# Feed-forward half of one trunk layer: output projection by chunks of 512 tokens, and three groups of the up projection begun with one chunk's products

## The chip, the cores and the metric

The kernel runs on one core of a Trainium2 chip. The metric is the device time of one execution in microseconds: 2342.04 us, the median of 3 runs (2341.98 to 2343.08). The engines are named as the profile names them: PE multiplies matrices into PSUM (8 banks of 128 x 512 float32), DVE and ACT work element by element, SP issues the DMAs, POOL does almost nothing here.

## The reference, cut to what is computed

One layer (`DEPTH = 1`) over 2048 latent tokens of width 1024: a bidirectional RG-LRU mixer of width 1280, then a SwiGLU feed-forward network of width 2816. Everything is float32. What matters here is the end of the mixer and the network behind it:

```
y = (rec * gelu(h @ w_gate)) @ w_out                    # 1280 -> 1024, the output projection
x = x + mx[2] * y
h = rms_norm(x, norm_ffn_g) * (1 + mx[4]) + mx[3]
a, b = split(h @ ffn_w_gu)                              # 1024 -> 2 x 2816, the up projection
x = x + mx[5] * ((silu(a) * b) @ ffn_w_down)            # 2816 -> 1024, the down projection
```

## The kernel before, in words

Tensors are kept transposed: features on the 128 partitions, tokens along the free dimension. The 2048 tokens are four chunks of C = 512, numbered 0 to 3. A float32 product is made of three matmuls on split operands (`mm3`, lines 103 to 109): each operand is a high part, rounded by ACT (line 83), and a low part, the rest, subtracted by DVE (line 84). A pair of weight or data tiles of 128 x 1024 that is loaded and split this way is called a **unit** (`unit`, line 96): one load of 512 KB on SP's queue, one cast, one subtraction.

`sweep1` computes the mixer. `sweep2` (line 1003), to which the change is confined, handles the chunks in two **supers**, (3, 2) and then (1, 0). For the first super:

- `w_out` (line 831) is the output projection of both chunks together. For each half `dg` of the 8 feature tiles it takes 8 banks, 4 per chunk, and runs over 5 steps `j`; a step loads one unit of weights and one unit of input per chunk (`rows`, line 816), 30 units for the super. Each bank is then scaled and added to x on DVE (line 843), stored to `d_x1` and squared and summed for the norm (lines 847 to 851).
- `norm2_bc` (line 854) turns the sums of squares of one chunk into a broadcast row: four small matmuls, 15 tiny DVE operations, one diagonal, one matmul, one copy.
- `combos` (line 865), called for k = 0 to 3, reloads tiles k and k + 4 of both chunks from `d_x1`, scales them (line 881), and makes the seven operands T0 to T6 of a scheme that gets the two chunks' products with both halves of the features in seven products instead of eight. T0 and T1 depend on the first chunk alone, T2 on the second alone, T3 to T6 on both. Each has a high part (ACT, lines 890 and 893) and a low part (DVE, lines 891 and 894). Four differences are formed on DVE (lines 904 to 908).
- `up` (line 935) runs over 22 groups `f`. `up_weights` (line 914) loads two weight tiles, forms four sums of them and splits the results into four operand tiles. Each group has seven products of 12 matmuls, numbered as T, into three banks: `be` collects products 0, 5, 6 and 3, and is copied out by ACT after 0, 5 and 6 (s1, s2, s3); `ep` collects 4 and 2; `al` has product 1. The order in the code is 0, 4, 5, 1, 6, then product 0 of the next group, 3, 2. SiLU and two multiplications give the two chunks' activations, which go to `d_act`.
- Beside `up` of the first super, `back_units` finishes the mixer for chunks 1 and 0 after every second group (a hook), with activations that need other function tables. Beside `down` of the first super the combinations of the second super are made.

Then follow `down` for chunks 3 and 2, `up` of the second super without a hook, and `down` for chunks 1 and 0.

The order of the instructions of each engine is not written out by hand in `sweep2`: a list scheduler at compile time orders them by readiness and priority, and assigns buffers as they come free. Loads and splits of units and weights are given a priority 200 places ahead of their place in the code (`w_off`, line 1059). The buffers that matter: 4 raw tiles (`RAWS`, loads and weight sums), 6 operand tiles (`OPS`, split results), 10 `ld` tiles and 6 `e` tiles of 128 x 512, 28 T tiles, 8 PSUM banks.

Of the kernel before, what the change touches and what calls it, by code (L numbers as in the profile page):

```python
# [12 lines left out]
P = 128  # L13
# [6 lines left out]
T = 2048  # L20
# [11 lines left out]
WS = 9  # L32

# [11 lines left out]
class Trunk:  # L45
# [770 lines left out]
    def rows(self, ps, w_src, x_srcs, name, after=None):  # L816

        m = len(w_src)
        for j in range(m):
            w = self.unit(w_src[j], f"w{name}_{j}")  # L820
            for q, x_src in enumerate(x_srcs):
                x = self.unit(x_src[j].rearrange("p a t -> p (a t)"), f"x{name}_{j}_{q}")
                for i in range(4):
                    for a in range(2):
                        ws, xs = slice(a * C + i * P, a * C + (i + 1) * P), slice(a * C, (a + 1) * C)
                        self.mm3(ps[q][i], (w[0][:, ws], w[1][:, ws]), (x[0][:, xs], x[1][:, xs]),
                                 j == a == 0, j == m - 1 and a == 1)
            if after:
                after(j)

    def w_out(self, s):

        nc = self.nc
        acc = [self.tile2("acc", f"acc{c}") for c in s]
        for dg in range(2):
            ps = [[self.bank(f"ps_wo{c}_{dg}{i}") for i in range(4)] for c in s]
            self.rows(ps, [self.io["w_out"][dg, j] for j in range(NB // 2)], [self.d_rg[c] for c in s], f"o{s[0]}_{dg}")
            for q, c in enumerate(s):
                for i in range(4):
# [3 lines left out]
                    nc.vector.scalar_tensor_tensor(out=x1, in0=ps[q][i], scalar=self.modv[:, d : d + 1], in1=x1,  # L843
                                                   op0=ALU.mult, op1=ALU.add)
                    nc.sync.dma_start(self.d_x1[c][:, d, :], x1)
                    if d == 0:
                        nc.scalar.activation(acc[q], x1, AF.Square)
                    else:
                        sq = self.tile2("e", f"sq{c}_{d}")
                        nc.scalar.activation(sq, x1, AF.Square)  # L850
                        nc.vector.tensor_tensor(out=acc[q], in0=acc[q], in1=sq, op=ALU.add)
# [13 lines left out]
    def combos(self, s, k, bc):  # L865
# [3 lines left out]
        nc = self.nc  # L869
        v = nc.vector  # L870
        sh = lambda j: self.modv[:, 8 + j : 9 + j]
# [3 lines left out]
        x = {}  # L875
        for r in range(2):
            for q in range(2):
                j = k + 4 * r
                t = self.tile2("ld", f"x1n_{s[q]}_{j}")
                nc.sync.dma_start(t, self.d_x1[s[q]][:, j, :])  # L880
                v.scalar_tensor_tensor(out=t, in0=t, scalar=self.A2[:, j : j + 1], in1=bc[q],
                                       op0=ALU.mult, op1=ALU.mult)
                x[r, q] = t
        T = []

        def part(i, src, bias=None):
            t = self.hp.tile([P, 2, C], F32R, tag="T", name=f"T{s[0]}_{k}_{i}", bufs=28)
            h, l = t[:, 0, :], t[:, 1, :]
            if bias is None:
                nc.scalar.copy(h, src)  # L890
                v.tensor_tensor(out=l, in0=src, in1=h.bitcast(F32), op=ALU.subtract)
            else:
                nc.scalar.activation(h, src, AF.Identity, bias=bias, scale=1.0)
                v.scalar_tensor_tensor(out=l, in0=src, scalar=bias, in1=h.bitcast(F32),
                                       op0=ALU.add, op1=ALU.subtract)
            T.append(t)

        b1, b2 = sh(k), sh(k + 4)
        part(0, x[0, 0], b1)
        part(1, x[1, 0], b2)  # L900
        part(2, x[1, 1], b2)
        e = lambda n: self.tile2("e", f"{n}_{s[0]}_{k}")
        t1, t2, t4 = e("t1"), e("t2"), e("t4")
        v.tensor_tensor(out=t1, in0=x[0, 1], in1=x[0, 0], op=ALU.subtract)
        v.scalar_tensor_tensor(out=t2, in0=x[1, 1], scalar=b2, in1=t1, op0=ALU.add, op1=ALU.subtract)
        v.scalar_tensor_tensor(out=t4, in0=x[1, 0], scalar=b2, in1=t2, op0=ALU.add, op1=ALU.subtract)
        t3 = x[0, 1]
        v.scalar_tensor_tensor(out=t3, in0=x[1, 1], scalar=self.shd[:, k : k + 1], in1=t3,
                               op0=ALU.add, op1=ALU.subtract)
        for i, t in ((3, t4), (4, t1), (5, t2), (6, t3)):  # L910
            part(i, t)
        return T

    def up_weights(self, s, f):
# [4 lines left out]
        with self.tc.high_priority(offset=self.w_off):  # L919
# [4 lines left out]
            lo, hi = slice(0, C), slice(C, 2 * C)  # L924
            tt = v.tensor_tensor
            tt(out=sums[:, lo], in0=b[:, lo], in1=b[:, hi], op=ALU.add)
# [3 lines left out]
            pa, ps, pb = (self.parts(t, f"{n}{tag}") for n, t in (("a", a), ("s", sums), ("b", b)))  # L930
            p4 = self.parts(s4, f"s4{tag}", C)
        part = lambda t, o: (t[:, 0, o], t[:, 1, o])
        return [part(pa, lo), part(pa, hi), part(p4, lo), part(pb, hi), part(ps, lo), part(ps, hi), part(pb, lo)]

    def up(self, s, T, hook):
# [4 lines left out]
        v = nc.vector  # L940

        def product(ps, A, i, first):
            for k in range(4):
                ks = slice(k * P, (k + 1) * P)
                x = T[k][i]
# [3 lines left out]
        def add(t, ps):  # L949
            v.tensor_tensor(out=t, in0=ps, in1=t, op=ALU.add)  # L950
# [166 lines left out]
```

## Time and profile before

| | us |
|---|---|
| median of 3 runs | 2342.04 |
| the profiled execution | 2343.92 |
| its span, first to last instruction | 2342.2 |
| PE busy | 2253.5 |
| DVE busy | 1489.7 |
| ACT busy | 1156.4 |
| mean granted clock of PE (1 is full) | 0.975 |

The profiled execution is 1.88 us above the median, and its span 1.7 us shorter than its time. The first super's output projection runs from 721.6 to 836 us, its up projection to 1331, the second super's output projection to 1430, the two down projections to 1680, the second up projection to 2110, the last two down projections to the end. Busy time of PE is modelled from pipelined matmuls; how many were issued in a stretch, and the granted clock, say more than its share.

### The profile page before, as it was taken

To read this page: it belongs to the slowest core of one execution; us is meant where nothing else is said; L and a number is where in the kernel's file an instruction comes from. 1 tells how busy PE (TensorE), PEld (TensorE's weight loads), DVE (VectorE), ACT (ScalarE), POOL (GpSimd) and SP (SyncE) were. 2 spreads that over 40 slices of the span, in tenths; PEclk is the share of its full clock that TensorE was granted. 3 is DMA by queue.
4 is the path that set the end of the run, shared out by engine and by line. 5 is a ranking of instruction groups with operands and counts; after the bars stand their busy time and mean duration, and the time that the engine had idled before them with its cause. 6 is when DMAs were issued, how large, how long until landed. Compare 5 with 4: busy or idle time off the path is not lost.

```text
span 2342.2 us, 25844 instructions
## 1 busy us (share of the span) xinstructions
PE 2253.5 (96%) x9852; PEld 1852.4 (79%) x9852; DVE 1489.7 (64%) x1912; ACT 1156.4 (49%) x1399; POOL 0.7 (0%) x6
## 2 busy tenths in 40 slices
PE   8899999899999958999999999999999999999999
PEld 8578887688887846878787888778888888888887
DVE  4567888678887577676666546864555555545443
ACT  2357775687776335565646334443333333333332
POOL 0000000000000000000000000000000000000000
PEclk9799999999999978999999999999999999999999
DMA  7135555221114733434343666776422222236664
GB/s 280 41 140 207 204 178 207 85 73 63 63 63 154 250 127 112 150 127 164 126 163 121 204 227 225 242 263 232 162 81 81 81 81 81 87 129 224 227 215 143
DMA packets 126556, 356.23 MB, mean 152 GB/s; under 512 B 15072, under 2 KB 15072, under 8 KB 125408
## 3 DMA queue, kind: packets, MB, share of 16 engines
q1 hardware_dynamic: 126432, 354.58, 44.5%
q8 instruction: 77, 1.26, 0.2%
q14 instruction: 47, 0.39, 0.0%
HBM read 283.22 MB, written 71.30 MB: 151 GB/s over the span
## 4 chain that ended last, share of the span: by engine, by line
PE 68%; ACT 7%; DVE 3%; issue 2%; DMA 1%; SPq 0%; DVEq 0%; ACTq 0%
PE ps_dn L107 6%; PE ps_dn L108 6%; PE ps_dn L106 6%; PE ps_be L106 6%; PE ps_be L107 6%; PE ps_be L108 6%; PE ps_ep L108 3%; PE ps_ep L107 3%; PE ps_ep L106 3%; PE ps_wo L106 3%; PE ps_wo L107 3%; PE ps_wo L108 3%; ACT L77 2%; PE ps_rec L108 2%; PE ps_rec L107 2%
## 5 line engine op out<-in xcount | busy, mean ns | idle before, releaser
L107 PE MATMUL ps_dn<-op_xd,op_wd 128*128 128x512 f32 x704 | 275.2, 391 | 1.9 <-DVE op_xd L84 1.8
L108 PE MATMUL ps_dn<-op_xd,op_wd 128*128 128x512 f32 x704 | 274.7, 390 | 0.0
L106 PE MATMUL ps_dn<-op_xd,op_wd 128*128 128x512 f32 x704 | 270.4, 391 | 1.6 <-ACT op_xd L83 1.6
L84 DVE TENSOR_TENSOR op_wd<-raw_wd,op_wd 128x1024 fp32r<-128x1024 f32 x88 | 107.7, 1223 | 200.2 <-ACT op_wd L83 200.1
L83 ACT CAST op_wd<-raw_wd 128x1024 fp32r<-128x1024 f32 x88 | 92.7, 1053 | 270.1 <-PE ps_dn L108 221.1
L950 DVE TENSOR_TENSOR s<-ps_ep,s 128x512 f32<-128x512 f32 x88 | 60.6, 688 | 154.1 <-ACT s L975 104.9
L107 PEld LDWEIGHTS ps_dn<-op_xd,op_wd 128*128 128x128 f32 x704 | 132.6, 188 | 30.8 <-DVE op_xd L84 3.2
L106 PEld LDWEIGHTS ps_dn<-op_xd,op_wd 128*128 128x128 f32 x704 | 132.1, 188 | 30.2 <-ACT op_xd L83 2.4
L108 PEld LDWEIGHTS ps_dn<-op_xd,op_wd 128*128 128x128 f32 x704 | 132.7, 189 | 27.6
L106 PE MATMUL ps_be<-T,op_b 128*128 128x512 f32 x352 | 139.5, 396 | 9.5 <-ACT s L975 9.5
L77 ACT ACT_TABLE_LOAD x113 | 145.0, 1283 | 2.7 <-PEq L1109 0.7
L106 PE MATMUL ps_ep<-T,op_s 128*128 128x512 f32 x352 | 138.3, 394 | 8.3 <-ACT T L890 8.3
L108 PE MATMUL ps_be<-T,op_b 128*128 128x512 f32 x352 | 138.4, 393 | 0.0
L107 PE MATMUL ps_be<-T,op_b 128*128 128x512 f32 x352 | 138.2, 393 | 0.0
L387 DVE SCALAR_TENSOR_TENSOR u<-ps_rec,c_conv_w,u 128x1024 f32<-128x1024 f32 x60 | 77.1, 1285 | 95.2 <-ACT u L384 93.6
L107 PE MATMUL ps_ep<-T,op_s 128*128 128x512 f32 x352 | 137.4, 390 | 0.0
L108 PE MATMUL ps_ep<-T,op_s 128*128 128x512 f32 x352 | 137.4, 390 | 0.0
L108 PE MATMUL ps_gate<-hx,op_g 128*128 128x512 f32 x320 | 127.0, 397 | 5.5 <-DVE op_g L84 5.5
L106 PE MATMUL ps_rec<-hx,op_r 128*128 128x512 f32 x320 | 129.6, 405 | 2.1 <-ACT hx L306 2.1
L107 PE MATMUL ps_rec<-hx,op_r 128*128 128x512 f32 x320 | 129.4, 404 | 0.6 <-DVE hx L307 0.6
L975 ACT COPY s<-ps_be 128x512 f32<-128x512 f32 x44 | 25.6, 583 | 207.8 <-PE ps_be L108 207.8
L108 PE MATMUL ps_rec<-hx,op_r 128*128 128x512 f32 x320 | 127.7, 399 | 0.0
(256 smaller groups left out, 5380.4 us busy)
## 6 DMA issues: line engine op xcount, KB each, us to landing
raw_wd<-in_down SPq DMA_DIRECT2D x88, 512.0 KB, 3.6
raw_xd<-d_act SPq DMA_DIRECT2D x88, 512.0 KB, 4.6
raw_ga<-in_gu SPq DMA_DIRECT2D x44, 512.0 KB, 3.9
raw_gb<-in_gu SPq DMA_DIRECT2D x44, 512.0 KB, 4.3
d_act<-s SPq DMA_DIRECT2D x88, 256.0 KB, 3.5
raw_xo<-d_rg SPq DMA_DIRECT2D x40, 512.0 KB, 4.2
raw_mod<-in_mod_t SPq DMA_DIRECT2D x32, 512.0 KB, 5.4
x<-in_x_t SPq DMA_DIRECT2D x48, 256.0 KB, 5.7
```

Source lines behind the costliest of these rows:

```text
L77: return self.table(self.nc.scalar.activation(out, in_, func, bias=bias, scale=scale))
L83: nc.scalar.copy(t[:, 0, :], raw)
L84: nc.vector.tensor_tensor(out=t[:, 1, :], in0=raw, in1=t[:, 0, :].bitcast(F32), op=ALU.subtract)
L106: ins = mm(ps, w[0], x[0], start=first, stop=False, skip_group_check=shared)
L107: mm(ps, w[0], x[1], start=False, stop=False, skip_group_check=shared)
L108: mm(ps, w[1], x[0], start=False, stop=last, skip_group_check=shared)
L387: v.scalar_tensor_tensor(out=part, in0=ps, scalar=cw[:, i : i + 1], in1=part, op0=ALU.mult, op1=ALU.add)
L950: v.tensor_tensor(out=t, in0=ps, in1=t, op=ALU.add)
L975: nc.scalar.copy(s3, be)
```

## The change

The output projection is done chunk by chunk. In `w_out(c, together)` a chunk is projected either with both halves `dg` at once (8 banks, two weight units and one input unit per step) or one half after the other (4 banks each, and the input is read twice). For the first super, chunk 3 is projected together, its norm taken and `combos_first` called for k = 0 to 3 (T0 and T1 of each); then chunk 2 is projected one half after the other. `up_early` then runs products 0 and 1 and the first SiLU of groups 0, 1 and 2: group 0 with its whole weights, groups 1 and 2 with the split of the first weight tile alone, which is loaded again when `up_weights` makes the other operands. Then `combos_second` makes the remaining five operands for each k, in the order T4, T5, T6, T3, T2, from T0 and T1 rather than from the first chunk's tiles (an operation more for t1 and for t4 each), with its temporaries in raw tiles instead of `e` tiles. In the second super both chunks are projected together, and both halves of the combinations are called in a row at the place of the old ones.

In `up` the order within a group is now 0, 1, 5, 4, 6, product 0 of the next group, 3, 2 (group 0: 4 ahead of 5), and the multiplication with the first SiLU comes after the second SiLU. The splits in `up_weights` begin with the first tile's.

```diff
+EARLY = 3
...
+    def rows(self, ps, w_srcs, x_src, name, after=None):
+        m = len(x_src)
         for j in range(m):
+            w = [self.unit(src[j], f"w{name}_{j}_{g}") for g, src in enumerate(w_srcs)]
+            x = self.unit(x_src[j].rearrange("p a t -> p (a t)"), f"x{name}_{j}")
+            for g in range(len(w_srcs)):
...
+    def w_out(self, c, together):
+        acc = self.tile2("acc", f"acc{c}")
+        for dgs in ((0, 1),) if together else ((0,), (1,)):
+            ps = [[self.bank(f"ps_wo{c}_{dg}{i}") for i in range(4)] for dg in dgs]
...
+    def combos_first(self, s, k, bc):
+        T = {}
+        for r in range(2):
+            j = k + 4 * r
+            T[r] = self.t_tile(s, k, r)
+            self.operand(T[r], self.scaled(s[0], j, bc), self.modv[:, 8 + j : 9 + j])
+        return T
+
+    def combos_second(self, s, k, bc, T):
...
+        x01, x11 = self.scaled(s[1], k, bc), self.scaled(s[1], k + 4, bc)
+        t = self.wp.tile([P, 2, C], F32, tag="raw", name=f"t12_{s[0]}_{k}", bufs=RAWS)
+        t1, t2 = t[:, 0, :], t[:, 1, :]
+        t4 = self.wp.tile([P, 2, C], F32, tag="raw", name=f"t4_{s[0]}_{k}", bufs=RAWS)[:, 0, :]
+        v.scalar_tensor_tensor(out=t1, in0=x01, scalar=b1, in1=part(0, 0), op0=ALU.add, op1=ALU.subtract)
+        v.tensor_tensor(out=t1, in0=t1, in1=part(0, 1), op=ALU.subtract)
+        self.operand(T[4], t1)
+        v.scalar_tensor_tensor(out=t2, in0=x11, scalar=b2, in1=t1, op0=ALU.add, op1=ALU.subtract)
+        self.operand(T[5], t2)
...
+    def up_first(self, s, f):
+        with self.tc.high_priority(offset=self.w_off):
+            a = self.raw(self.io["gu"][f, 0], f"ge{s[0]}_{f}")
+            t = self.parts(a, f"e{s[0]}_{f}")
...
+    def up_head(self, s, f, A, T, be):
+        nc = self.nc
+        s1 = self.tile2("e", f"s1_{s[0]}_{f}")
+        nc.scalar.copy(s1, be)
+        al = self.bank(f"ps_al{s[0]}_{f}")
+        self.product(al, A, T, 1, True)
+        nc.vector.tensor_tensor(out=s1, in0=al, in1=s1, op=ALU.add)
+        self.act(s1, s1, AF.Silu)
+        return s1
+
+    def up_early(self, s, T, n):
+        A = [self.up_weights(s, 0)] + [self.up_first(s, f) for f in range(1, n)]
+        early = []
+        for f in range(n):
+            be = self.up_begin(s, f, A[f], T)
+            early.append((A[f], be, self.up_head(s, f, A[f], T, be)))
+        return early
...
         s = supers[0]
-        for c, acc in zip(s, self.w_out(s)):
-            bc[c] = self.norm2_bc(c, acc)
+        bc[s[0]] = self.norm2_bc(s[0], self.w_out(s[0], True))
+        T = [self.combos_first(s, k, bc[s[0]]) for k in range(4)]
+        acc = self.w_out(s[1], False)
+        bc[s[1]] = self.norm2_bc(s[1], acc)
+        early = self.up_early(s, T, EARLY)
         for k in range(4):
-            prepare(s, k)
+            self.combos_second(s, k, bc[s[1]], T[k])
...
-        self.up(s, T.pop(s), beside_up)
+        self.up(s, T, beside_up, early)
         s2 = supers[1]
-        accs = self.w_out(s2)
+        accs = [self.w_out(c, True) for c in s2]
```

## Rows read from the trace of the kernel before

**Rows 1.** The page, parts 1 and 2: PE's busy line, slices, granted clock

```profile
PE 2253.5 (96%) x9852; PEld 1852.4 (79%) x9852; DVE 1489.7 (64%) x1912; ACT 1156.4 (49%) x1399; POOL 0.7 (0%) x6
...
PE   8899999899999958999999999999999999999999
...
PEclk9799999999999978999999999999999999999999
```

**Rows 2.** Windows: stretch, length, busy (xcount) per engine, PEclk, DMA share, GB/s

```profile
740.00:750.00 10.00, 10.00 (x46) 8.27 (x45) 9.96 (x10) 2.18 (x3) 0.00 (x0) 1.00 0.39 127
840.00:860.00 20.00, 5.76 (x19) 4.56 (x20) 15.74 (x46) 2.29 (x4) 0.00 (x0) 0.50 0.53 178
860.00:880.00 20.00, 12.74 (x38) 8.67 (x38) 17.59 (x28) 9.38 (x16) 0.00 (x0) 0.64 0.25 74
880.00:900.00 20.00, 15.84 (x49) 10.88 (x48) 19.86 (x31) 10.17 (x16) 0.00 (x0) 0.74 0.33 110
890.00:900.00 10.00, 10.00 (x34) 7.84 (x34) 9.90 (x16) 7.22 (x11) 0.00 (x0) 0.76 0.24 79
```

**Rows 3.** Windows over whole stages, same columns

```profile
835.90:860.70 24.80, 6.84 (x22) 4.74 (x21) 19.84 (x52) 5.64 (x8) 0.00 (x0) 0.59 0.49 163
860.70:905.00 44.30, 31.75 (x102) 22.30 (x101) 40.24 (x61) 21.15 (x35) 0.00 (x0) 0.73 0.28 88
782.00:836.00 54.00, 54.00 (x240) 44.62 (x238) 28.57 (x34) 18.94 (x22) 0.00 (x0) 1.00 0.57 194
1432.00:1550.00 118.00, 114.50 (x497) 92.56 (x496) 95.93 (x140) 57.91 (x73) 0.00 (x0) 0.99 0.74 253
1680.00:2080.00 400.00, 400.00 (x1766) 331.24 (x1765) 211.59 (x270) 133.03 (x187) 0.00 (x0) 1.00 0.27 89
```

**Rows 4.** Timeline of PE: start, us, what, idle before and its releaser

```profile
835.89 0.39 PE L108 MATMUL ps_wo<-op_xo,op_wo 128*128 128x512 f32 x1
...
859.68 2.07 PE L142 MATMUL n_bc<-n_diag,ones 128*128 128x512 f32 x2 [7.40 <-DVE n_diag L138]
...
860.76 1.41 PE L106 MATMUL ps_be<-T,op_a 128*128 128x512 f32 x1
```

**Rows 5.** Timeline of DVE, same columns: first norm, scalings, last low part

```profile
844.38 0.15 DVE L123 TENSOR_SCALAR rstd_m<-ss_ps 128x4 f32<-128x4 f32 x1
...
847.96 0.69 DVE L138 TENSOR_TENSOR n_diag<-ident,rstd_y 128x512 f32<-128x512 f32 x1
...
851.44 3.40 DVE L881 SCALAR_TENSOR_TENSOR x1n<-x1n,A_ffn,bcn 128x512 f32<-128x512 f32 x5 [2.79 <-ACT bcn L148]
...
862.41 3.40 DVE L881 SCALAR_TENSOR_TENSOR x1n<-x1n,A_ffn,bcn 128x512 f32<-128x512 f32 x5 [2.79 <-ACT bcn L148]
...
895.85 0.68 DVE L891 TENSOR_TENSOR T<-x1n,T 128x512 fp32r<-128x512 f32 x1
```

**Rows 6.** Timelines of ACT and DVE: weight tiles made behind the projection

```profile
836.32 1.04 ACT L83 CAST op_a<-raw_ga 128x1024 fp32r<-128x1024 f32 x1 [0.44 <-PE ps_wo L108]
...
841.85 1.22 DVE L84 TENSOR_TENSOR op_s<-s,op_s 128x1024 fp32r<-128x1024 f32 x1
```

**Rows 7.** The page, part 5: subtraction and cast of one unit

```profile
L84 DVE TENSOR_TENSOR op_wd<-raw_wd,op_wd 128x1024 fp32r<-128x1024 f32 x88 | 107.7, 1223 | 200.2 <-ACT op_wd L83 200.1
L83 ACT CAST op_wd<-raw_wd 128x1024 fp32r<-128x1024 f32 x88 | 92.7, 1053 | 270.1 <-PE ps_dn L108 221.1
```

**Rows 8.** PE's waits (us, times, longest), 905 to 1313 and 715 to 730

```profile
PE ps_be L106 <- ACT s L975: 9.5, 9, 2.3
PE ps_be L106 <- ACT op_a L83: 4.3, 1, 4.3
...
PE ps_wo L106 <- ACT r L77: 2.0, 1, 2.0
```

**Rows 9.** DMA issues from 905 to 1313; timeline of SP's queue

```profile
raw_gb<-in_gu SPq DMA_DIRECT2D x19, 512.0 KB, 4.5
...
846.92 31.40 SPq L880 DMA_DIRECT2D x1n<-d_x  x7
```

More of the change, by code (lines that the diff above doesn't have):

```diff
@@ L863, in norm2_bc, with operand, scaled, t_tile @@
         return self.bc_sbuf(self.spread(y, f"n2_{c}"), f"n2_{c}")
[L865 to L871, printed above, removed]
+    def operand(self, t, src, bias=None):
+        h, l = t[:, 0, :], t[:, 1, :]
+        if bias is None:
+            self.nc.scalar.copy(h, src)
+            self.nc.vector.tensor_tensor(out=l, in0=src, in1=h.bitcast(F32), op=ALU.subtract)
+        else:
+            self.nc.scalar.activation(h, src, AF.Identity, bias=bias, scale=1.0)
+            self.nc.vector.scalar_tensor_tensor(out=l, in0=src, scalar=bias, in1=h.bitcast(F32),
+                                                op0=ALU.add, op1=ALU.subtract)
+    def scaled(self, c, j, bc):
+        t = self.tile2("ld", f"x1n_{c}_{j}")
+        self.nc.sync.dma_start(t, self.d_x1[c][:, j, :])
+        self.nc.vector.scalar_tensor_tensor(out=t, in0=t, scalar=self.A2[:, j : j + 1], in1=bc,
+                                            op0=ALU.mult, op1=ALU.mult)
+        return t
+    def t_tile(self, s, k, i):
+        return self.hp.tile([P, 2, C], F32R, tag="T", name=f"T{s[0]}_{k}_{i}", bufs=28)
+    def combos_first(self, s, k, bc):
[6 more added lines that the diff above has]
+    def combos_second(self, s, k, bc, T):
+        v = self.nc.vector
         if k == 0:
@@ L884, in combos @@
[L884 to L896, printed above, removed]
@@ L924, in up_weights @@
             lo, hi = slice(0, C), slice(C, 2 * C)
+            part = lambda t, o: (t[:, 0, o], t[:, 1, o])
             tt = v.tensor_tensor
+            if head is None:
+                pa = self.parts(a, f"a{tag}")
+                head = [part(pa, lo), part(pa, hi)]
             tt(out=sums[:, lo], in0=b[:, lo], in1=b[:, hi], op=ALU.add)
@@ new lines, in product, with up_begin @@
+    def product(self, ps, A, T, i, first):
+        for k in range(4):
+            ks = slice(k * P, (k + 1) * P)
+            x = T[k][i]
+            self.mm3(ps, (A[i][0][:, ks], A[i][1][:, ks]), (x[:, 0, :], x[:, 1, :]),
+                     first and k == 0, k == 3, shared=True)
+    def up_begin(self, s, f, A, T):
+        be = self.bank(f"ps_be{s[0]}_{f}")
+        self.product(be, A, T, 0, True)
+        return be
+    def up_head(self, s, f, A, T, be):
[7 more added lines that the diff above has]
+        return s1
@@ L939, in up @@
+    def up_early(self, s, T, n):
[5 more added lines that the diff above has]
+        return early
+    def up(self, s, T, hook, early=()):
         nc = self.nc
         v = nc.vector
[L942 to L945, printed above, removed]
-                self.mm3(ps, (A[i][0][:, ks], A[i][1][:, ks]), (x[:, 0, :], x[:, 1, :]),
-                         first and k == 0, k == 3, shared=True)
@@ L949, in add, with weights @@
-        def add(t, ps):
-            v.tensor_tensor(out=t, in0=ps, in1=t, op=ALU.add)
-        A, banks = {}, {}
+        add = lambda t, ps: v.tensor_tensor(out=t, in0=ps, in1=t, op=ALU.add)
+        W = {f: e[0] for f, e in enumerate(early)}
+        be = {f: e[1] for f, e in enumerate(early)}
+        s1 = {f: e[2] for f, e in enumerate(early)}
+        def weights(f):
+            if f < NF and len(W.get(f, ())) < 7:
+                W[f] = self.up_weights(s, f, W.get(f))
         def begin(f):
-            A[f] = self.up_weights(s, f)
-            banks[f] = self.bank(f"ps_be{s[0]}_{f}")
-            product(banks[f], A[f], 0, True)
+            if f < NF and f not in be:
+                be[f] = self.up_begin(s, f, W[f], T)
@@ L959, in up @@
+        weights(0)
         begin(0)
@@ L992, in down @@
             ps = [self.bank(f"ps_dn{c}_{dg}{i}") for i in range(4)]
-            self.rows([ps], [io["down"][dg, j] for j in range(NF // 2)], [self.d_act[c]], f"d{c}_{dg}",
+            self.rows([ps], [[io["down"][dg, j] for j in range(NF // 2)]], self.d_act[c], f"d{c}_{dg}",
                       (lambda j: after(dg, j)) if after else None)
```

112 lines of the change are left out of this document (46 added, 66 removed).

## The prediction

> **What bounds the kernel now.** Read the page first. PE is busy 96% of the span, and of the 40 slices few are below 9: the opening, and two neighbours near the middle (5 and 8), where the granted clock drops too [rows 1]. So PE sets the time nearly everywhere, and a change can win only where PE stands idle or runs slowly. Next come the windows over that place. A full stretch issues 46 matmuls in 10 us [rows 2], and a long undisturbed one 1766 in 400 us [rows 3], which makes 0.2265 us per 128x512 matmul. After 835.9 us, the last matmul of the output projection [rows 4], the counts fall to 19, 38 and 49 in three stretches of 20 us [rows 2], where 88 would fit. From 860.7 to 905, when PE runs freely again, there are 102, worth 23.1 us; before 860.7 stand only the small ones of the norms [rows 3]. So 24.8 + 44.3 - 23.1 = **46.0 us are lost in this stage**.
>
> What ends the waits? The PE timeline shows a chain: PE reaches the second norm's broadcast at 859.7 and the first up product at 860.8 [rows 4]. Behind it stands DVE: it begins to scale one chunk at 851.4 and the other at 862.4, and its last low part starts at 895.9 [rows 5]; from 880 to 900 it is busy 19.9 of 20 us [rows 2]. So the stage has two parts: 25 us of chain, in which PE has nothing to do, and some 35 us of DVE work, in which PE gets its operands in drops.
>
> **The change part by part.** (1) *PE gets work for the chain.* Chunk 3 is finished first, and its T0 and T1 are made while chunk 2 is projected. Groups f = 0, 1, 2 do products 0 and 1: 3 x 2 x 12 = 72 matmuls, 16.3 us, ready at 835.9. Their weights hide beside them: today too a tile beyond group 0's is cast at 836.3, and the second such one's subtraction ends at 843.1 [rows 6]; groups 1 and 2 take the same two buffers, and group 0's and 1's matmuls (5.4 us each) cover both. Without that cover each would cost its cast and subtraction, 2.3 us.
>
> (2) *DVE's share after the chain.* One norm chain is left, ready at 851.4 as the first is now. Then the second half of the combinations needs per k 2 scalings, 2 operations for t1, one each for t2 and t3, 2 for t4 and 5 low parts: 13 (15 before; with the 4 moved ahead 17). Five in a row take 3.40 us, so (3.40 - 0.74) / 4 = 0.66 us from one to the next, 0.74 being the duration of the last alone. 52 x 0.66 = 34.3, and 3 additions for the heads make 36.3 us: DVE ends at 887.7. Six operations of the last k (4.0 us) follow T5, so at 883.7 there remain of group 0 some 42 matmuls: products 6, 3, 2 and the last quarters of 4 and 5. At the 34 per 10 us of the stretch nearest to this one [rows 2] they take 12.4 us, to 896.1. By then PE has done 72 + 60 = 132 matmuls, 29.9 us, so 60.2 - 29.9 = 30.3 are lost. **Gain 46.0 - 30.3 = 15.7 us.** At best groups 1 and 2 also run products 4 and 5 of k = 0 to 2 beside DVE (36 matmuls, 8.2 us) and the end runs at full clock (42 x 0.2265 = 9.5 instead of 12.4): 26.8. At worst nothing is gained (rivals).
>
> On the clock, rows first: the granted clock is 0.50 from 840 to 860, 0.64 and 0.74 in the next two stretches [rows 2], that is, largely the 1.2 GHz level, after PE had gone short of work. The matmuls there mostly waited for DVE, so I price only the last 42. The Trainium skill, "TensorE: Matmul & The Clock Gate", section "Terms", prices throttled time at that time x (1 - K/N): the 45 us at half clock that these rows make would be an estimate of 22 us, and 16 us of busy PE could give back 8 of them beyond my sum. The trace does not bear that out for the sparse part, where a faster clock would only have waited longer.
>
> (3) *Crowding while chunk 2 is projected.* In 54 us DVE is busy 28.6 [rows 3]. Added: 5 more units (chunk 2 reads its input twice, 20 units for 15) x 1.22 = 6.1 [rows 7]; the first norm, 4.3 (844.4 to 848.7) [rows 5]; the first half of the combinations, 16 x 0.66 = 10.6. Sum 49.6 of 54. ACT, busy 18.9 of 54 there, has room for 5 casts of 1.05 and 8 short ones. The nearest row is the down projection with the combinations beside it: DVE 95.9 of 118, and PE lost 118 - 497 x 0.2265 = 5.4 us [rows 3]. I take **+2** (0 to 6): stalls of PE here only move the start of a stage whose end DVE sets.
>
> (4) *The beginning of the output projection* needs two weight tiles and then the input, one unit more: a cast and a subtraction, 1.05 + 1.22 at most [rows 7]. PE waits 2.0 us there for an activation that reads sweep 1's banks [rows 8], which hides part: **+1** (0 to 2.3).
>
> (5) *Second super.* The output projection has 30 units as before: 0. The combinations beside down have 17 operations per k instead of 15: 8 x 0.66 = 5.3 us on DVE, to 101.2 of 118; and t1, t2, t4 now sit in the 4 raw buffers that the loads use. The results are due only at 1680, so much can slip: **+2** (-4, if the buffers spread them out, to +8).
>
> (6) *Order inside up.* Product 1 comes ahead of 5, and 4 behind it. Each snapshot copy of `be` still has one product (2.7 us) beside it; the multiply by the first SiLU moves behind the second and holds one of 8 banks longer. In the first up PE loses 9.5 us to nine copies and 4.3 to one cast that stand in ACT's queue [rows 8]; the same back units stay. **0** (-5 to +5). The second up loses nothing [rows 3], and DVE, busy 211.6 of 400 us, goes on covering its operands.
>
> (7) *Queues.* SP issues 2 more weight tiles (the first halves of groups 1 and 2 are loaded again) and 5 more units, and eight x1n loads move ahead of chunk 2's. At 4.5 us to landing [rows 9] and a DMA share of 0.57 in that window [rows 3] I cost them at nothing while the raw buffers turn over; otherwise see the last rival. POOL's queue is not passed.
>
> Sum: -15.7 + 2 + 1 + 2 + 0 = -10.7. The profiled execution took 2343.9 us, 1.9 above the median of 2342.0: 2333.2 there, **2331.3 as a median**.
>
> **Rivals.** *Filled shadow.* The later groups run beside DVE and PE keeps its clock: a gain of 26.8 instead of 15.7, so 2320. For it: a product needs only its T and weights, and six banks suffice. Against: today only group 0's products stand before 901, and group 2's other weights need buffers that group 0 holds until its end. The page's price of the clock would point this way.
>
> *DVE is the end anyway.* Chunk 3's operands slip behind 835.9, since DVE is at 92% before it; then the early products start late, and the combinations later by as much. All 10.6 us of them slipped cancel the gain: 2342. For it: DVE is full in the tail. The compiler orders each engine's queue, and could put the early products elsewhere, so that the change would not do what it says, with the same result.
>
> *Raw buffers.* Temporaries of the combinations share four buffers with loads that are scheduled ahead of them. A load waiting for a buffer stands on SP's queue before x1n loads; that this queue stands is visible today (7 issues over 31.4 us) [rows 9]. A k that waits for one turnover loses 4.5 + 1.05 + 1.22 = 6.8 us; two of four cost 13.6 and more than cancel the 10.7; three give 2331.3 + 20.4 = 2352. It decides from the second wait on. Against: DVE's own 13 operations on one k (8.6 us) cover one turnover.
>
> **Numbers.** Forecast 0.50 (its own range 2324 to 2337), filled shadow 0.20, DVE anyway 0.16, raw buffers 0.14. About 0.2% (4.7 us) can be told from no change here: faster 0.70, same 0.16, slower 0.14. The range reaches up to two raw waits (2345) and down past the filled shadow by the good ends of (5) and (6): 2313 to 2346.
>
> **What would show it.** Right: 72 matmuls without a pause after the projection's last one, one norm broadcast in that time instead of two, DVE full from some 851 to 888, and 30 us lost instead of 46. Wrong: gaps in the projection of chunk 2 ended by DVE (3); waits of x1n or t1 for raw buffers, or SP standing with loads behind it (last rival); more than 14 us lost to ACT's queue in the first up (6); more than 7 beside down (5).

## The result, and the profile after

The change makes the kernel slower: 2376.57 us, the median of 4 runs (2373.71 to 2379.55), against 2342.01 (2341.79 to 2343.08). The ratio is 1.0147 with an interval of 1.0129 to 1.0164. The profiled execution took 2373.71 us with a span of 2371.9, so 29.7 us more than before are to be found in the trace. It is the fastest of the four: the spans of the others are 2373.0, 2376.5 and 2377.8. Line numbers have moved a little: L106 to L108 of before are L107 to L109 now, the casts L84, the subtractions L85, the scaling L886, the norm's sums L855 and L864.

The page's parts 1 and 2, after, answer to [rows 1]:

```profile
PE 2257.3 (95%) x9852; PEld 1851.8 (78%) x9852; DVE 1498.0 (63%) x1933; ACT 1162.2 (49%) x1404; POOL 0.7 (0%) x6
...
PE   8899999899998878999999998899999999999999
...
PEclk9799999999999988999999999899999999999999
```

The hole of two slices near the middle (5 and 8) is now four shallower ones (8, 8, 7, 8), and there is a new one of two slices (8, 8) ten slices later, in the first down projection. To see how much each stage gained or lost I count its matmuls as the prediction does: length of the stage minus matmuls x 0.2265 us. The table is worked out in this way from all matmul records; the boundaries lie at the first or last matmul of a kind.

| us lost by PE | before | after | difference |
|---|---|---|---|
| mixer | 133.7 | 134.3 | +0.6 |
| output projection, first half (before) / chunk 3 (after) | 5.8 | 5.3 | -0.5 |
| output projection, second half / chunk 2 | 0.0 | 13.7 | **+13.7** |
| 70 us behind the projection's last matmul | 45.3 | 28.1 | **-17.2** |
| rest of the first up projection | 20.6 | 38.8 | **+18.2** |
| second output projection | 0.1 | 0.1 | 0 |
| first down projection, combinations beside it | 9.4 | 23.4 | **+14.0** |
| second up projection | 0.3 | 1.3 | +1.0 |
| all the rest | 4.2 | 4.3 | +0.1 |

The sum is 29.9, the span's 29.7. So the place for which the change was costed did get better, by 17.2 us, and three others got worse by 45.9. The windows of after say the same; columns as in [rows 2]:

```profile
782.00:849.70 67.70, 57.99 (x248) 47.46 (x248) 48.91 (x72) 29.63 (x37) 0.00 (x0) 0.92 0.68 229
850.23:862.00 11.77, 2.89 (x11) 2.28 (x10) 8.43 (x23) 3.04 (x4) 0.00 (x0) 0.68 0.69 223
862.00:880.00 18.00, 18.00 (x73) 14.23 (x72) 15.94 (x25) 8.79 (x15) 0.00 (x0) 0.92 0.00 0
880.00:919.30 39.30, 31.40 (x108) 21.78 (x107) 32.09 (x49) 16.00 (x25) 0.00 (x0) 0.78 0.44 141
1445.00:1563.00 118.00, 101.29 (x436) 81.46 (x435) 93.89 (x144) 52.79 (x66) 0.00 (x0) 0.93 0.64 217
```

Chunk 2's projection takes 67.7 us where the second half took 54 for the same 240 matmuls [rows 3]; the down projection's 118 us hold 436 matmuls instead of 497 [rows 3].

**Where each wait is.** The timeline of PE, after (start, us, what, idle before it and its releaser):

```profile
787.97 1.87 PE L864 MATMUL ss_ps<-ones,acc 128*128 128x1 f32 x8 [5.95 <-DVE acc L855]
...
793.60 2.08 PE L143 MATMUL n_bc<-n_diag,ones 128*128 128x512 f32 x2 [3.77 <-DVE n_diag L139]
794.69 1.42 PE L107 MATMUL ps_wo<-op_xo,op_wo 128*128 128x512 f32 x1
...
850.16 0.39 PE L109 MATMUL ps_wo<-op_xo,op_wo 128*128 128x512 f32 x1
855.66 1.87 PE L864 MATMUL ss_ps<-ones,acc 128*128 128x1 f32 x8 [5.11 <-DVE acc L855]
861.29 2.08 PE L143 MATMUL n_bc<-n_diag,ones 128*128 128x512 f32 x2 [3.77 <-DVE n_diag L139]
862.38 1.42 PE L107 MATMUL ps_be<-T,op_a 128*128 128x512 f32 x1
...
886.30 0.80 PE L107 MATMUL ps_ep<-T,op_s 128*128 128x512 f32 x1 [2.86 <-ACT T L876]
```

The two norms stand in PE's queue ahead of work that is ready: chunk 3's ahead of chunk 2's projection, chunk 2's ahead of the early products. PE waits for the norm's inputs (5.95 and 3.77 us, then 5.11 and 3.77) and takes nothing from behind meanwhile. The order of PE's matmuls there in the trace, counted by destination (the digit is the chunk or the group):

```
240 ps_wo | ss_ps | n_3_bc | 240 ps_wo | ss_ps | n_2_bc | 12 be_0 | 12 al_0 | 12 be_1 | 12 al_1 | 12 be_2 | 12 al_2 | 3 ep_0 ...
```

So the early products don't cover the chain behind the projection (850.2 to 862.4, PE nearly idle) but run behind it, from 862.4 to 880, without a pause: 73 matmuls in 18 us. The timeline of DVE in the same place shows its share, first scaling and last low part:

```profile
864.03 5.39 DVE L886 SCALAR_TENSOR_TENSOR x1n<-x1n,A_ffn,bcn 128x512 f32<-128x512 f32 x8 [2.79 <-ACT bcn L149]
...
899.98 0.75 DVE L880 SCALAR_TENSOR_TENSOR T<-x1n,modv,T 128x512 fp32r<-128x512 f32 x1
```

In the first up projection it is `op_a`, the first operand tile of the next group, that comes late. PE's waits (us in all, times, longest) from 922 to 1345, after; they answer to [rows 8]:

```profile
PE ps_be L107 <- ACT op_a L84: 16.4, 7, 2.9
PE ps_be L109 <- DVE op_a L85: 5.1, 5, 3.1
PE ps_be L107 <- ACT s L1028: 2.4, 2, 1.7
```

One such wait on ACT's timeline, and the matmul on PE's that waits for it:

```profile
1077.67 1.28 ACT L78 ACT_TABLE_LOAD   x1
1078.97 1.15 ACT L78 ACTIVATE bg<-bg 128x512 f32<-128x512 f32 x2
1080.14 1.28 ACT L78 ACT_TABLE_LOAD   x1
1081.43 0.72 ACT L78 ACTIVATE ba<-br,c_a 128x512 f32<-128x512 f32 x1
1082.06 1.03 ACT L84 CAST op_a<-raw_ga 128x1024 fp32r<-128x1024 f32 x1
```

```profile
1083.14 0.79 PE L107 MATMUL ps_be<-T,op_a 128*128 128x512 f32 x1 [2.89 <-ACT op_a L84]
```

The cast of the next group's first tile stands in ACT's queue behind 4.4 us of the hook's table loads and activations. Before, at the same point of the group, that cast was long done, and the tile cast in the middle of the hook was the last one of a group, `op_s` of 128x512 for product 2 (1078.67). ACT's and PE's timelines, before:

```profile
1066.37 1.05 ACT L83 CAST op_a<-raw_ga 128x1024 fp32r<-128x1024 f32 x1 [1.24 <-issue]
...
1074.28 1.28 ACT L77 ACT_TABLE_LOAD   x1
```

```profile
1074.29 0.39 PE L106 MATMUL ps_be<-T,op_a 128*128 128x512 f32 x1
```

In the first down projection one pause stands out. The page's part 5, then ACT's, SP's and DVE's timelines, all after:

```profile
L107 PE MATMUL ps_dn<-op_xd,op_wd 128*128 128x512 f32 x704 | 272.2, 392 | 14.9 <-ACT op_xd L84 14.9
```

```profile
1478.14 0.59 ACT L149 COPY bcn<-n_bc 128x512 f32<-128x512 f32 x1 [6.43 <-PE n_bc L143]
1482.92 0.62 ACT L876 CAST T<-t 128x512 fp32r<-128x512 f32 x1 [4.19 <-DVE t L917]
...
1485.29 1.04 ACT L84 CAST op_wd<-raw_wd 128x1024 fp32r<-128x1024 f32 x1
...
1489.62 1.03 ACT L84 CAST op_xd<-raw_xd 128x1024 fp32r<-128x1024 f32 x1
```

```profile
1474.20 0.36 SPq L91 DMA_DIRECT2D raw_wd<-in_down  x1
1474.66 0.37 SPq L91 DMA_DIRECT2D raw_xd<-d_act  x1
1486.04 0.33 SPq L91 DMA_DIRECT2D raw_wd<-in_down  x1
```

```profile
1485.33 0.68 DVE L877 TENSOR_TENSOR T<-t,T 128x512 fp32r<-128x512 f32 x1
```

The step's two loads go out at 1474 and have landed, by the trace, at 1480.4 and 1481.6, but ACT casts them at 1485 and 1489, the first behind the casts of T4, T5 and T6, of which T4's waits 4.19 us for DVE's t1, the second also behind the cast of T3 and three activations (L879); the longest wait of PE is 12.6 us. So the loads come late, and the casts come later still. The next load goes out 11.4 us after the one before it: t1 and t2 share one raw tile and t4 has another, and it goes out at 1486.04, as DVE's last read of the first (T5's low part, above) ends.

### The profile page after: what moved, and what is told of

It is laid out like the page before. It is cut to its first block, busy times and chain, and to the rows that moved or that the text cites. A ratio compares the mean times of both kernels' runs of the same rounds, so it can differ in the third digit from the quotient of the medians.

```text
span 2371.9 us, 25859 instructions
## 1 busy us (share of the span) xinstructions
PE 2257.3 (95%) x9852; PEld 1851.8 (78%) x9852; DVE 1498.0 (63%) x1933; ACT 1162.2 (49%) x1404; POOL 0.7 (0%) x6
## 4 chain that ended last, share of the span: by engine, by line
PE 62%; DVE 8%; ACT 6%; DMA 4%; issue 2%; SPq 0%; DVEq 0%; ACTq 0%
PE ps_dn L108 6%; PE ps_dn L109 6%; PE ps_dn L107 6%; PE ps_be L109 5%; PE ps_be L107 5%; PE ps_be L108 5%; PE ps_wo L107 3%; PE ps_wo L108 3%; PE ps_wo L109 3%; DMA raw_gb<-in_gu 3%; PE ps_ep L107 2%; PE ps_ep L109 2%; PE ps_ep L108 2%; ACT L78 2%; PE ps_rec L107 2%
## 5 line engine op out<-in xcount | busy, mean ns | idle before, releaser
L107 PE MATMUL ps_dn<-op_xd,op_wd 128*128 128x512 f32 x704 | 272.2, 392 | 14.9 <-ACT op_xd L84 14.9
L108 PE MATMUL ps_dn<-op_xd,op_wd 128*128 128x512 f32 x704 | 274.9, 390 | 0.1
L109 PE MATMUL ps_dn<-op_xd,op_wd 128*128 128x512 f32 x704 | 274.6, 390 | 0.0
L85 DVE TENSOR_TENSOR op_wd<-raw_wd,op_wd 128x1024 fp32r<-128x1024 f32 x88 | 107.7, 1223 | 189.8 <-ACT op_wd L84 189.6
L84 ACT CAST op_wd<-raw_wd 128x1024 fp32r<-128x1024 f32 x88 | 92.7, 1053 | 246.4 <-PE ps_dn L109 204.4
L84 ACT CAST op_s<-s 128x1024 fp32r<-128x1024 f32 x88 | 73.7, 837 | 235.8 <-PE ps_be L109 170.9
L107 PEld LDWEIGHTS ps_dn<-op_xd,op_wd 128*128 128x128 f32 x704 | 132.8, 189 | 43.7 <-ACT op_xd L84 16.2
L108 PEld LDWEIGHTS ps_dn<-op_xd,op_wd 128*128 128x128 f32 x704 | 132.6, 188 | 28.7 <-DVE op_xd L85 1.2
L109 PEld LDWEIGHTS ps_dn<-op_xd,op_wd 128*128 128x128 f32 x704 | 132.6, 188 | 27.6
L107 PE MATMUL ps_be<-T,op_b 128*128 128x512 f32 x352 | 139.8, 397 | 6.2 <-ACT s L1024 3.2
L107 PE MATMUL ps_ep<-T,op_s 128*128 128x512 f32 x352 | 137.9, 392 | 5.2 <-ACT T L876 4.6
L108 PE MATMUL ps_be<-T,op_b 128*128 128x512 f32 x352 | 138.8, 394 | 0.0
L109 PE MATMUL ps_be<-T,op_b 128*128 128x512 f32 x352 | 138.6, 394 | 0.0
L108 PE MATMUL ps_ep<-T,op_s 128*128 128x512 f32 x352 | 137.7, 391 | 0.8 <-DVE T L877 0.8
L109 PE MATMUL ps_ep<-T,op_s 128*128 128x512 f32 x352 | 137.4, 390 | 0.0
L107 PE MATMUL ps_rec<-hx,op_r 128*128 128x512 f32 x320 | 129.6, 405 | 2.1 <-ACT hx L307 2.1
L109 PE MATMUL ps_gate<-hx,op_g 128*128 128x512 f32 x320 | 126.2, 395 | 5.5 <-DVE op_g L85 5.5
L108 PE MATMUL ps_rec<-hx,op_r 128*128 128x512 f32 x320 | 129.5, 405 | 0.5 <-DVE hx L308 0.5
L107 PE MATMUL ps_wo<-op_xo,op_wo 128*128 128x512 f32 x320 | 123.5, 395 | 4.7 <-ACT r L78 3.3
L109 PE MATMUL ps_rec<-hx,op_r 128*128 128x512 f32 x320 | 128.0, 400 | 0.0
```

The lines of the kernel that those rows point to most:

```text
L84: nc.scalar.copy(t[:, 0, :], raw)
L85: nc.vector.tensor_tensor(out=t[:, 1, :], in0=raw, in1=t[:, 0, :].bitcast(F32), op=ALU.subtract)
L107: ins = mm(ps, w[0], x[0], start=first, stop=False, skip_group_check=shared)
L108: mm(ps, w[0], x[1], start=False, stop=False, skip_group_check=shared)
L109: mm(ps, w[1], x[0], start=False, stop=last, skip_group_check=shared)
```

## The experiments

The theory after this reading: three side effects cost 46 us, each by the order of an in-order queue, and the idea itself is worth 17. "after" is the changed kernel; lines with - and + are edits to it. e1 to e5 were timed once each, and the executions of after alone differ by 5.9 us in span, so their stages say more than their totals. A line "stages" gives the loss, as in the table above, of: chunk 2's projection | 70 us behind it | rest of the first up | first down. For after it is 13.7 | 28.1 | 38.8 | 23.4.

**e1_late_norm3: chunk 3's norm taken after two steps of chunk 2's projection.**

```diff
-        bc[s[0]] = self.norm2_bc(s[0], self.w_out(s[0], True))
-        T = [self.combos_first(s, k, bc[s[0]]) for k in range(4)]
-        acc = self.w_out(s[1], False)
+        acc3 = self.w_out(s[0], True)
...
+            if j == 1:
+                bc[s[0]] = self.norm2_bc(s[0], acc3)
+                T.extend(self.combos_first(s, k, bc[s[0]]) for k in range(4))
...
+        acc = self.w_out(s[1], False, beside_second)
```

> Only edit: chunk 3's norm and the first half of the combinations are called after step 1 of chunk 2's projection instead of ahead of it. Theory (PE's queue: the norm's few matmuls stood ahead of chunk 2's, and PE waited for their inputs from 781.6 to 794.7): PE goes on without a pause, its loss there falls from 13.3 us to under 2, and the span of 2371.9 falls by 9 to 13 us. Rival (DVE sets the end anyway): the norm is then some 10 us later, chunk 3's operands are late for the early products, the 13 us come back behind the projection, and the span falls by less than 4.

Measured: 2377.08 us, span 2375.2. Stages: 1.4 | 33.1 | 48.4 | 24.1. The two waits at the chunks' border are gone, as the window over chunk 2's projection shows (56 us full, at full clock, with the norm inside):

```profile
782.00:838.00 56.00, 56.00 (x251) 46.15 (x250) 45.33 (x69) 27.96 (x35) 0.00 (x0) 1.00 0.73 253
```

That step cost 12.3 us, shown. Of these 5.0 come back behind the projection, where the first scaling now comes 18.3 us after the projection's last matmul instead of 13.9. The total went the other way (3.3 us of span), because the first up projection, which this edit doesn't touch, lost 9.6 us more; that is taken up below.

**e2_norm2_between: chunk 2's norm split in two, between the early groups, so that PE has their products during the chain.**

```diff
-        bc[s[1]] = self.norm2_bc(s[1], acc)
-        early = self.up_early(s, T, EARLY)
+        early = self.up_early(s, T, EARLY, (
+            lambda: y.append(self.norm2_rstd(s[1], acc)),
+            lambda: bc.__setitem__(s[1], self.norm2_rest(s[1], y[0]))))
```

> Only edit: chunk 2's norm is called in two parts, behind the early products of group 0 and of group 1, instead of ahead of all of them. Theory (PE's queue): the 12.1 us that PE stood between 850.2 and 862.3 are filled with the early products, and the span of 2371.9 falls by about 12 us. Rival (DVE sets the end of this stage): the early products only move from beside DVE's combinations to beside the norm, PE then starves where they were, DVE ends its combinations at the same time after the projection as now (50 us), and the span falls by less than 3.

Measured: 2384.18 us, span 2382.4. Stages: 13.7 | 27.6 | 50.2 | 22.7. PE did get its early products during the chain, and then stood without work instead:

```profile
850.63 0.39 PE L107 MATMUL ps_be<-T,op_a 128*128 128x512 f32 x1
...
862.41 1.02 PE L143 MATMUL n_bc<-n_diag,ones 128*128 128x512 f32 x2
...
872.51 0.80 PE L107 MATMUL ps_ep<-T,op_s 128*128 128x512 f32 x1 [3.62 <-ACT T L881]
...
898.52 0.80 PE L107 MATMUL ps_be<-T,op_b 128*128 128x512 f32 x1 [1.72 <-ACT s L1031]
```

and in after:

```profile
899.33 0.80 PE L107 MATMUL ps_be<-T,op_b 128*128 128x512 f32 x1 [1.73 <-ACT s L1024]
```

Product 6 of group 0 (`ps_be<-T,op_b`), which follows product 5 and so the last of the combinations' T5, begins at 898.5 here and at 899.3 in after, and DVE ends its last low part at 900.4 here and 900.7 in after: DVE sets the end of the stage, and the early products only move within it. So the wrong place of the products, though real, costs nothing in this stage. The total is 10.5 us of span longer, since the first up projection, untouched here too, lost 11.4 us more.

**e3_old_order: the products of a group in the old order, and the multiplication in its old place.**

```diff
-            if f not in s1:
-                s1[f] = self.up_head(s, f, w, T, b)
...
-            if f == 0:
-                self.product(ep, w, T, 4, True)
...
+            self.product(ep, w, T, 4, True)
             self.product(b, w, T, 5, False)
             nc.scalar.copy(s2, b)
-            if f > 0:
-                self.product(ep, w, T, 4, True)
+            if head:
...
+                self.product(al, w, T, 1, True)
...
+            v.tensor_tensor(out=a, in0=b, in1=a, op=ALU.mult)
```

> Only edit: the products within a group of the up projection go back to the order before (0, 4, 5, 1, 6, next 0, 3, 2) and the first multiplication to its place behind product 3; groups 0 to 2 keep their early products 0 and 1. Theory (product order: product 1 at the head of a group gives its operand tile back earlier and the other tiles later, so that the next group's first tile is cast only behind the back units' table loads): the loss in the first up, 38 us between 920 and 1341, falls to about 20, the span by 15 to 19. Rival (the place where the first tile is split, or the early groups' weights): the loss stays above 33 and the span falls by less than 5.

Measured: 2351.19 us, span 2349.2, 22.7 less. Stages: 13.7 | 28.1 | 17.6 | 22.7. The first up's loss is even below that of before (20.6), and its waits on the cast of `op_a` are gone.

**e4_e_temps: t1, t2 and t4 of the second super in e tiles, as before.**

```diff
+        if s[0] == 1:
+            t1, t2, t4 = (self.tile2("e", f"{n}_{s[0]}_{k}") for n in ("t1", "t2", "t4"))
+        else:
             t = self.wp.tile([P, 2, C], F32, tag="raw", name=f"t12_{s[0]}_{k}", bufs=RAWS)
```

> Only edit: in the second super t1, t2 and t4 lie in e tiles again instead of raw tiles (the first super keeps raw tiles). Theory (raw buffers: the temporaries take three of the four raw tiles, the loads of the down projection come late, and the casts of its units stand behind casts that wait for DVE): the pause of 12.6 us behind the second norm's broadcast in the first down projection goes, its loss falls from 23 to about 9 us, and the span by 12 to 15. Rival (the two halves called in a row, or 17 operations instead of 15): the pause stays and the span falls by less than 4.

Measured: 2353.82 us, span 2352.0, 19.9 less. Stages: 15.1 | 28.8 | 37.0 | 2.8. The same 118 us of the down projection, windows of this kernel:

```profile
1426.00:1544.00 118.00, 118.00 (x526) 97.24 (x525) 96.62 (x142) 56.19 (x68) 0.00 (x0) 1.00 0.76 253
```

DVE does as much as in after (96.6 against 93.9 us), and PE issues 526 matmuls instead of 436. So the operations more for t1 and t4 cost nothing; the raw tiles cost it all. That the loss falls below before's 9.4 wasn't expected, and its reason wasn't sought.

**e5_parts_mult: the new order of products, but the order of the splits in `up_weights` and the multiplication as before.**

```diff
-            if head is None:
-                pa = self.parts(a, f"a{tag}")
...
             tt(out=s4, in0=a[:, hi], in1=sums[:, hi], op=ALU.subtract)
+            if head is None:
+                pa = self.parts(a, f"a{tag}")
...
+            a = s1.pop(f)
+            v.tensor_tensor(out=a, in0=b, in1=a, op=ALU.mult)
...
             self.product(ep, w, T, 2, False)
...
-            a = s1.pop(f)
-            v.tensor_tensor(out=a, in0=b, in1=a, op=ALU.mult)
```

> The other two edits inside up are undone and the new product order kept: the first weight tile is split behind the sums again, and the first multiplication stands behind product 3 again. Theory (product order alone makes the loss in the first up): the loss there stays at 36 to 50 us (38.8 in the changed kernel), with waits for the cast of op_a of some 3 us after the back units. Rival (one of these two made it): the loss falls below 25 us and the span of 2371.9 by 13 or more.

Measured: 2381.78 us, span 2380.0. Stages: 15.0 | 28.8 | 45.2 | 24.0. With e3 this leaves the order of the products alone as the cause of the first up's 18 us. How it acts is seen in the distance from the end of each cast of `op_a` to the first matmul of product 0, which uses it. From the fifth such cast of the stage on it is 8.2 to 9.9 us before, 4.2 to 6.9 in e3, and 0.1 to 3.6 in after and in e5. Under the new order nothing is left to cover a hook that stands in front of the cast. Why the cast comes so late under it is not shown: products 0 and 1 use `op_a`, 4 and 5 the second tile, 6 and 3 the third, 2 the fourth, so the order sets when each of the 6 operand tiles comes free, but more tiles were not tried.

**Why the first up's loss varies under the new order.** From windows over that stage, PE's idle time is its length minus busy time, and the rest is what the busy time exceeds matmuls x 0.2265:

| | window | matmuls | idle | excess of busy | clock |
|---|---|---|---|---|---|
| before | 408 | 1713 | 13.7 | 6.3 | 0.99 |
| after | 423 | 1699 | 26.7 | 11.5 | 0.98 |
| e4 | 423 | 1706 | 26.5 | 10.1 | 0.99 |
| e1 | 425 | 1665 | 27.8 | 20.1 | 0.96 |
| e2 | 423 | 1649 | 28.2 | 21.3 | 0.95 |
| e5 | 423 | 1671 | 25.6 | 19.0 | 0.96 |
| e3 | 413 | 1748 | 13.2 | 3.9 | 1.00 |

Three of these windows, of before, after and e3, columns as above:

```profile
905.00:1313.00 408.00, 394.26 (x1713) 322.50 (x1712) 273.75 (x371) 229.57 (x304) 0.00 (x0) 0.99 0.44 148
```

```profile
922.00:1345.00 423.00, 396.34 (x1699) 321.38 (x1698) 268.56 (x367) 226.78 (x299) 0.00 (x0) 0.98 0.44 146
```

```profile
922.00:1335.00 413.00, 399.82 (x1748) 326.80 (x1747) 276.98 (x372) 230.35 (x302) 0.00 (x0) 1.00 0.45 153
```

The new order doubles the idle time in all five kernels that have it alike (25.6 to 28.2). What varies is what the low clock behind the pauses costs: 10 to 11.5 us of slow matmuls in two, 19 to 21 in the others. Why these differ is open. It need not lie in the edits: the execution of after that is read here has a mean clock of 0.975, as e4's, and the other three of the same kernel 0.968 to 0.972 at spans longer by 1.1 to 5.9 us; e1, e2 and e5 have 0.967 to 0.970. Either way it swallowed e1's gain.

**c1_order_temps, c2_late3, c3_all: the edits together.** c1 has those of e3 and e4, c2 also that of e1, c3 also that of e2.

```diff
+        if s[0] == 1:
+            t1, t2, t4 = (self.tile2("e", f"{n}_{s[0]}_{k}") for n in ("t1", "t2", "t4"))
...
+            self.product(ep, w, T, 4, True)
             self.product(b, w, T, 5, False)
...
+                bc[s[0]] = self.norm2_bc(s[0], acc3)
```

> The two edits that worked alone together: old product order in up, and e tiles for the temporaries of the second super. The rest of the change stays. If the two add up (22.7 and 19.9 us of span), the span is 2371.9 - 42.6 = 2329.3, a ratio of about 0.9945 to the kernel before; the first half of the change then gains 45.3 - 28.1 = 17 us behind the projection and pays 13.7 for chunk 3's norm. Rival (they overlap, since a stall that goes only uncovers the next): the span stays above 2338.

> The kernel with old product order and e tiles, and chunk 3's norm called after step 1 of chunk 2's projection. Theory (the 12 us won there were hidden in the single run of this edit by a first up that came out 10 us worse under the new product order): with the old order they show, less the 5 us that the later operands cost behind the projection: span 2321 to 2324, ratio 0.991 to 0.992. Rival (DVE sets the end anyway, what is won at 781 comes back): within 3 us of the kernel without this edit.

> The same with chunk 2's norm between the early groups as well. In the single run of that edit the loss behind the projection was 27.6 against 28.1 us, so it should be worth nothing while DVE ends the stage: within 2 us of the kernel without it. Rival (PE's queue counts there too, and something else gave it back): 8 us or more faster than that kernel.

| | median, us | ratio to before | span | stages |
|---|---|---|---|---|
| c1 | 2333.73 | 0.9961 (0.9947 to 0.9975) | 2332.5 | 15.3, 29.0, 18.2, 2.8 |
| c2 | 2325.03 | 0.9923 (0.9909 to 0.9938) | 2322.2 | 1.4, 33.3, 17.4, 2.8 |
| c3 | 2327.80 | 0.9936 (0.9921 to 0.9951) | 2325.7 | 1.4, 35.8, 18.6, 2.8 |

The effects nearly add up: 2371.9 - 22.7 - 19.9 = 2329.3 for c1, measured 2332.5. Without the disturbed up projection the late norm is worth 10.3 us of span in the profiled executions (c1 to c2) and 8.7 by the medians. The norm between the early groups gains nothing here either: c3 is 2.8 us slower than c2 by the medians, a little more than the 2 us expected, and loses 2.5 us more behind the projection. c2 beats both kernels. Of the 20.0 us of span that it gains on the kernel before, 12.0 lie behind the projection, where the idea was to pay; 6.6 are the first down projection's lower loss, whose reason was not sought, and 3.2 the first up's, less 1.4 for chunk 2's projection.

**d0_early0, d1_early1, c2_again: c2 with no early group, with one, with three.**

```diff
-EARLY = 3
+EARLY = 1
...
-        early = self.up_early(s, T, EARLY)
+        early = []
```

(The first pair of lines is d1, the second d0.)

> c2_late3 with one early group instead of three (EARLY = 1). Theory, that DVE ends the stage behind the projection and PE has room beside it: the 48 early products of groups 1 and 2 are done later, at 0.2265 us each, 10.9 us, less up to 2.4 us because DVE splits two weight tiles fewer in that time. Loss behind the projection 33.3 + 8.5 to 10.9 = 42 to 44 us, span 2322.2 + 8.5 to 10.9 = 2331 to 2333. Rival, that the early products only move work and the gain is the one norm chain alone: loss 33 us and span within 3 us of 2322.2.

> c2_late3 without the early groups (EARLY = 0), so that of the idea only chunk 3's operands made beside chunk 2 are left. Theory: group 0's products 0 and 1 need nothing but T0 and T1 and are taken by PE as soon as they are ready, with or without the loop of early groups, so this is worth the same as one early group: span 2331 to 2333. Rival, that without the loop PE gets to group 0 only behind the combinations: 24 matmuls more are late, 5.4 us, span 2336 to 2339.

> c2_late3 once more, on the chip of the two kernels with fewer early groups: span 2322.2 within 3 us.

Measured on one chip: c2 again 2324.84 us (ratio 0.9926, 0.9912 to 0.9941; span 2323.8), d1 2327.40 (0.9937, 0.9922 to 0.9952; span 2327.8), d0 2343.37 (1.0003, 0.9994 to 1.0013; span 2342.3). Behind the projection they lose 32.6, 39.2 and 45.1 us. So groups 1 and 2 bring 6.6 us in that stage, below the 8.5 to 10.9 of the theory, and 4.0 in the span of the profiled executions, 2.6 by the medians. Part of the reason is on DVE's timeline: with three groups the first scaling comes 18.1 us after the projection's last matmul, with one 15.6, and two weight tiles' subtractions of 1.2 us stand ahead of it.

d0 missed both expectations: without the loop the whole gain is gone. Its timelines of PE, ACT and SP:

```profile
879.14 0.79 PE L107 MATMUL ps_be<-T,op_a 128*128 128x512 f32 x1 [30.25 <-ACT op_a L84]
```

```profile
877.53 0.61 ACT L876 CAST T<-x1n 128x512 fp32r<-128x512 f32 x1
878.05 1.04 ACT L84 CAST op_a<-raw_ga 128x1024 fp32r<-128x1024 f32 x1
```

```profile
873.87 0.33 SPq L91 DMA_DIRECT2D raw_ga<-in_gu  x1
```

DVE begins to scale sooner than in the other two (11.3 us after the projection's last matmul), but group 0's weights are loaded only at 873.9.

**d3_early0_e: d0 with the first super's t1, t2 and t4 in e tiles too.**

```diff
-        if s[0] == 1:
+        if True:
             t1, t2, t4 = (self.tile2("e", f"{n}_{s[0]}_{k}") for n in ("t1", "t2", "t4"))
```

> d0_early0 with t1, t2 and t4 of the first super in e tiles as well, so that no temporary of the combinations takes a raw tile. Theory, that the 30.25 us for which PE stands on group 0's first cast there come from the temporaries, which take all four raw tiles ahead of the weights' loads (the load is issued at 873.9): the load goes out before 845, PE begins with group 0 right behind the norm's broadcast near 848, the loss behind the projection falls from 45.1 to that of one early group, 39 us, and the span from 2342.3 to 2328 to 2333. Rival, that the weights come late because the combinations stand ahead of them in the code, whatever tiles they use: load near 874 again, span within 3 us of 2342.

Measured: 2334.85 us, ratio 0.9969 (0.9958 to 0.9981), span 2331.1, and 39.6 us lost behind the projection, the theory's numbers. SP's timeline:

```profile
834.84 0.33 SPq L91 DMA_DIRECT2D raw_ga<-in_gu  x1
```

So the temporaries in raw tiles held up the weights in d0, as they held up the units of the down projection. And with that out of the way, one norm chain instead of two and T0, T1 beforehand are worth 5.7 us behind the projection (45.3 to 39.6). c2, with its early groups, loses 7.0 us less again there; it differs from d3 in the temporaries' tiles too.

## Why the prediction was wrong

The forecast was 2331.3 us, the measurement 2376.57; the sign was wrong, and the range (up to 2346) didn't hold it.

- **Steps (1) and (2), the gain behind the projection, were right in size**: 15.7 us forecast, 17.2 measured; a loss of 30.3 forecast, 28.1 measured. DVE's share was 36.3 us by the sum and 36.7 by the trace (864.03 to 900.73). But the picture was wrong in one point: the 72 products were to come right behind the projection's last matmul and came 12.2 us later, behind the norm. e2 shows why the number held all the same: the sum took the end of the stage from DVE, and DVE sets it.
- **Step (3) failed**: +13.7 us instead of +2. It took chunk 3's norm as 4.3 us of DVE's time. The norm also has matmuls, and these stand in PE's queue ahead of chunk 2's 240: PE waits 5.95 us for the sums of squares and 3.77 for the diagonal, and its granted clock there is low (0.92 over the stage). The step's clause that a stall here only moves the start of a stage whose end DVE sets was half right: of the 12.3 us that e1 took away, 5.0 came back behind the projection, and in c2 4.3 of 13.9.
- **Step (4)**: -0.5 us instead of +1, half a us below its range.
- **Step (5) failed**: +14.0 instead of +2, beyond its bound of +8. It named the raw tiles, and priced DVE's operations, which e4 shows to cost nothing. What it missed: the temporaries hold back the loads, and with the loads late, casts of T that wait for DVE stand on ACT ahead of the cast of a unit that PE needs.
- **Step (6) failed**, and by most: +18.2 instead of 0, beyond +5. It looked at how long each snapshot copy is covered and at the banks; it didn't ask where the next group's casts would fall in ACT's queue: `op_a` is ready 0.1 to 3.6 us ahead of its product instead of 8.2 or more. The threshold that it gave for being wrong was 14 us of waits on ACT; the trace has 16.4 on `op_a` alone.
- **Step (7)**: two weight tiles and five units more on SP show no cost of their own; chunk 2's projection runs without a pause in e1 with all of them.
- **The rivals.** Filled shadow did not happen, and e2 and c3 show that it couldn't by a better place of the products. DVE anyway: its remark that the compiler could put the early products elsewhere came true, its result did not. Raw buffers had the mechanism and the sign, but its place was behind the first projection and its price up to 20 us on SP's queue; it struck in the down projection, by late loads and ACT's order, for 14 us, and behind the first projection only where the early loop was taken away (d0, 30.25 us). It was given 0.14.
- **On the clock**, the rows of after show 0.78 where there was 0.73 and 0.74 [rows 2, 3], but the part fed by DVE does not follow it: over 880 to 919.3 e2's clock is 0.71 against after's 0.78, and its product 6 begins 0.8 us sooner. The Trainium skill, "TensorE: Matmul & The Clock Gate", section "Terms", prices throttled time at that time x (1 - K/N). d1 and d3 bear on it: their mean clocks over the 70 us behind the projection are 0.71 and 0.78, by that rule an estimate of 4.9 us between them, and they lose 39.2 and 39.6 us. So the price does not show in this pair, where PE waits for operands; the two kernels differ in more than the clock, so it is no proof. In the first up projection the rule holds roughly: 0.96 over e1's 425 us would be an estimate of 17 us, and the excess of busy time is 20.1.

## What to carry to other kernels

Before moving a small dependent step (a norm, a broadcast) ahead of a long run of ready matmuls, look where its own matmuls fall in PE's queue: two waits for them cost 12 us here. Placing the norm two steps later took these away, and gave 5 back where DVE ended the next stage. Reordering products, or letting temporaries share a pool with loads, changes when buffers come free, and so the order of casts on another engine; cost it by asking, tile by tile, who frees what before whom. A stage that DVE feeds was not shortened here by giving PE its other work earlier within it (e2, c3); it was by more PE work whose operands were ready beforehand (d1 to c2, 6.6 us behind the projection).

## What the runs showed that was not expected

A pause of 3 us on PE costs more than itself. Windows of 4 us around the wait at 1083.14, after:

```profile
1079.00:1083.00 4.00, 1.25 (x6) 0.72 (x4) 0.99 (x2) 3.97 (x6) 0.00 (x0) 1.00 0.18 66
1083.00:1087.00 4.00, 3.86 (x10) 3.10 (x11) 1.22 (x1) 3.94 (x7) 0.00 (x0) 0.57 0.40 112
1087.00:1091.00 4.00, 4.00 (x20) 3.29 (x19) 3.02 (x5) 3.90 (x6) 0.00 (x0) 1.00 0.07 24
```

In the 4 us from the end of the pause the granted clock is 0.57, so mostly the 1.2 GHz level, and 10 matmuls are issued where 17 would fit: 1.6 us on top of a pause of 2.9. Over the whole first up projection this excess was 10 to 11.5 us beside some 27 of idle time in e4 and after, and 19 to 21 beside 26 to 28 in e1, e2 and e5.
